# Two-layer hybrid encoder: the last head's result stays on chip, and attention gets its own large tiles

## The chip, the cores and the metric

The kernel runs on one core of one Trainium2 chip. The metric is the device time of one execution in microseconds (us); three timed runs of the kernel before gave 2697.81 as the median, 2691.86 and 2702.72 as the ends. The profile is of one further execution.

## The reference

The input `h` has 256 tokens of 2048 channels. Two layers are computed, each with its own float32 weights:

```
u = rmsnorm(h);  z = u @ w_in                        # 6528 columns, shared out among four mixers
mix = concat[A(z_A), B(z_B), C(z_C), D(z_D)]         # 4 x 512 channels
h += mix @ w_out                                     # 2048 x 2048
h += relu(rmsnorm(h) @ w_up)^2 @ w_down              # 2048 x 8192 and back
h += (p[i] @ w_ple) * sigmoid(rmsnorm(h) @ w_gate)
```

A is differential attention: 4 heads, two 256x256 softmax maps a head, queries and keys normed. B is a gated linear recurrence in both directions, 4 heads of 128 channels. C is mean pooling with windows 2, 4, 8 and 16 and a small linear map. D is RWKV-7 time mixing in both directions, 8 heads of 64.

## The kernel before

All activations lie transposed, channels on the 128 partitions and the 256 tokens along the free dimension, so 2048 channels are 16 chunks of 128x256. A chunk of the 16 that `w_out` multiplies is one mixer output: chunks 0 to 3 are A's heads, 4 to 7 B's, 8 to 11 C's, 12 to 15 D's pairs of heads. Below, A3 is head 3 of A, and so on.

**Matrix products.** Each is done in split form: a float32 operand becomes a rounded part and a remainder. `wsplit` (L142 to L146) loads 128x1024 weights into a tile `raw` by a DMA on SyncE's queue (SP), ScalarE copies them to `wh` (L144), VectorE subtracts to get `wl` (L146). `split` (L180, L181) does the same for an activation. TensorE then runs three products (`mm3`, L151 to L153) or, where one of 512 columns holds two, two (`mm2`, L158, L159).

**Stages of a layer.** `mixers` (L395) computes z block by block (`K.z`, 51 blocks of 128 columns; L227 takes each from PSUM) and the four mixers. In the text of the program come first D's first part for four pairs, `invert`, D's second part for pairs (1, 3), then (0, 2), and then for c = 0 to 3 C's group, A's head and B's head (`rest`). Each finished chunk goes to DRAM with `put` (L413, a DMA on SP's queue) into `o_scr`.

**`w_out`.** `MIX` lists the order of the 16 chunks. The first 12 are loaded back (`load_mix`, L270 into `ot`, then split into `mh`) and used by the first product (`w_out1`, 16 blocks of 12 chunks, L158 and L159 with `mh`; L162 and L163 add to `h`). The last 4 are used by a second product (`w_out2`, L151 to L153 with `mh`, added at L305), into a tile `mh2` that takes the place of `u1`, the input of the z blocks.

**Memory.** A pool is a stretch of on-chip memory with named tiles; tiles with one tag share the place and follow one another. `dp` and `ab` hold the mixers' tiles. A and B share tags in `ab`: A's `qn`, B's `bQ` and its queries are tag `bQ`; A's `L` and B's `bK` are `x22`; A's `ct` and B's `bAT` are `x21`; both `vt` are `x13`; A's raw keys and B's `sg` are `x11`. So A of head c+1 waits with these tiles for B of head c, and B of head c+1 for A of head c+1. A and B also share two PSUM banks (`K.pab`), D has four (`K.pds`). At block 9 of the first product (`m == 9`) `dp` and `ab` are closed and a pool `wide` takes their place, with three buffers each of `raw`, `wh` and `wl` for all blocks from there on; blocks 0 to 8 use four `raw` and two each of the others in pool `wp`. A tile of `wide` waits for the tiles that lay at its place.

**Order.** The instructions of each engine, and DMAs of SP's queue, are put in order when the program is built, by a planner that simulates times and takes what is ready, earlier program text first. On the chip each queue runs in this order; an instruction that waits holds up what is behind it in the same queue.

Of the kernel before, what the change touches and what calls it, by code (L numbers as in the profile page):

```python
# [8 lines left out]
F32 = mybir.dt.float32  # L9
F32R = mybir.dt.float32r  # L10
# [6 lines left out]
P = 128  # L17
# [33 lines left out]

POOL_W = (2, 4, 8, 16)

MIX = [8, 0, 4, 9, 1, 5, 10, 15, 2, 13, 6, 11, 14, 3, 12, 7]
NOUT1 = 12
A_OFF, H_OFF, C_OFF, R_OFF = 0, 1536, 4096, 4608

# [14 lines left out]
def trunk(ctx: ExitStack, tc: tile.TileContext, xT, pT, w_in, w_out1, w_out2, w_up, w_down, w_gate, w_ple, pvec,  # L72
# [182 lines left out]
    for l in range(DEPTH):  # L255
# [32 lines left out]
        for m in range(KC):  # L288
# [4 lines left out]
                K.raw_bufs, K.w_bufs = RAW_WIDE, W_WIDE  # L293
            ps = out_block(w_out1[l, m], mh1, NOUT1, mm2)
            add_to(h[:, m], ps)
        mh2 = K.up.tile([P, KC - NOUT1, 2 * S], F32R, tag="u1", name="mh2")
        mh2 = [mh2[:, k] for k in range(KC - NOUT1)]
        for k in range(NOUT1, KC):
            load_mix(mh2[k - NOUT1], k)
        pgw = wide.enter_context(tc.tile_pool(name="pgw", bufs=4, space=PSUM, reuse_waits="tile"))  # L300
        K.accum = lambda name: pgw.tile([P, 512], F32, tag="accw", name=name)
# [1 line left out]
        for m in range(KC):  # L303
            ps = out_block(w_out2[l, m], mh2, KC - NOUT1, mm3)
            V.tensor_tensor(h[:, m], h[:, m], ps[:, :S], ALU.add)  # L305
            split(u[:, m], h[:, m], pc(l, "mlpg", m))
        op_.__exit__(None, None, None)
        K.up_.__exit__(None, None, None)


# [84 lines left out]
def mixers(K):  # L395
    nc, tc, l, es = K.nc, K.tc, K.l, K.es
    df_ = tc.tile_pool(name="df", bufs=1, side="right", reuse_waits="tile")
    K.df = df_.__enter__()
    D = MixerD(K)
    if l == 0:  # L400
        nc.sync.dma_start(K.cst, K.consts)
    else:
        nc.sync.dma_start(K.hscr, K.h)
    dp = es.enter_context(tc.tile_pool(name="dp", bufs=1, reuse_waits="tile"))
    ab = es.enter_context(tc.tile_pool(name="ab", bufs=1, reuse_waits="tile"))
    pd = es.enter_context(tc.tile_pool(name="pd", bufs=1, space=PSUM, reuse_waits="tile"))
    K.dp, K.ab, K.pd = dp, ab, pd
    K.pds = lambda name: pd.tile([P, 512], F32, tag="m", name=name, bufs=D_BANKS)
    K.pab = lambda name: pd.tile([P, 512], F32, tag="n", name=name, bufs=6 - D_BANKS)
    oscr = nc.dram_tensor("o_scr_%d" % l, (KC, P, S), F32, kind="Internal").ap()  # L410

    def put(chunk, t):
        nc.sync.dma_start(oscr[chunk], t)  # L413
    K.put = put

    def rest(c, base):
        K.base = base
        mixer_c(K, c)
        if l == 0 and c == 0:
            prepare(K)  # L420
        mixer_a(K, c)
        mixer_b(K, c)
    for c in range(4):
        D.first(c, 3 + 3 * c)
    df_.__exit__(None, None, None)
    D.invert()
    d2_ = tc.tile_pool(name="d2", bufs=1, side="right", reuse_waits="tile")
    K.d2 = d2_.__enter__()
    for cs in ((1, 3), (0, 2)):
        D.second(cs)  # L430
    d2_.__exit__(None, None, None)
    for c in range(4):
        rest(c, 15 + 9 * c)
    return oscr
# [450 lines left out]
def mixer_c(K, gi):  # L885
    nc, tc, l, ab, pd = K.nc, K.tc, K.l, K.ab, K.pd
    V, A, G, T = nc.vector, nc.scalar, nc.gpsimd, nc.tensor
    PW = 8 + S + 8
    cw = ab.tile([P, P], F32, tag="cw", name="cw", bufs=2)
    nc.sync.dma_start(cw, K.cw[l, :, gi])  # L890
    zt = ab.tile([P, PW], F32, tag="zc", name="zc", bufs=1)
    G.memset(zt[:, 0:8], 0.0)
    G.memset(zt[:, 8 + S:], 0.0)
    K.z(K.base, zt[:, 8:8 + S])
    cur, lo_, n = zt, 0, PW

    for st in range(gi + 1):
        nxt = ab.tile([P, PW], F32, tag="zs", name="zs", bufs=2)
        a_, b_ = (1, 0) if st == 0 else (1 << (st - 1), 1 << (st - 1))
        lo2, n2 = lo_ + a_, n - a_ - b_  # L900
        G.tensor_tensor(nxt[:, lo2:lo2 + n2], cur[:, lo2 - a_:lo2 - a_ + n2], cur[:, lo2 + b_:lo2 + b_ + n2],
                        ALU.add)
        cur, lo_, n = nxt, lo2, n2
    dd = ab.tile([P, S], F32, tag="zd", name="zd", bufs=1)
    ic = ICN + gi * 16
    G.tensor_scalar(dd[:, 8:S - 8], cur[:, 16:S], 1.0 / POOL_W[gi], None, ALU.mult)
    G.tensor_tensor(dd[:, 0:8], cur[:, 8:16], K.cst[:, ic:ic + 8], ALU.mult)
    G.tensor_tensor(dd[:, S - 8:], cur[:, S:S + 8], K.cst[:, ic + 8:ic + 16], ALU.mult)
    G.tensor_tensor(dd, dd, zt[:, 8:8 + S], ALU.subtract)
    pw = K.pab("psc")  # L910
    T.matmul(pw[:, :S], cw, dd, start=True, stop=True)
    V.tensor_scalar(dd, pw[:, :S], K.pc(l, "cb", gi), K.pc(l, "cs", gi), ALU.add, ALU.mult)
    K.put(8 + gi, dd)


def mixer_a(K, h):
    nc, tc, l, ab, pd = K.nc, K.tc, K.l, K.ab, K.pd
    V, A, G, T = nc.vector, nc.scalar, nc.gpsimd, nc.tensor
    mat, pc, dcol = K.mat, K.pc, K.dcol

    def t1(tag="t1", bufs=3, name=None):
        return ab.tile([P, S], F32, tag=tag, name=name or tag, bufs=bufs)

    for x, gn in ((0, "aq"), (1, "ak")):
        t = t1("x1%d" % x, 1)
        K.z(K.base + 1 + x, t)
        sq = t1()
        A.activation(sq, t, AF.Square)
        p2 = K.pab("psa1")
        T.matmul(p2[:, :S], mat("bo64"), sq, start=True, stop=True)  # L930
        rs = t1()
        K.rsqrt(rs, p2[:, :S], K.eps_b)
        if x == 0:

            qn = ab.tile([P, 2, S], F32, tag="bQ", name="qn")
            for m in range(2):
                V.scalar_tensor_tensor(qn[:, m], t, pc(l, gn, m), rs, ALU.mult, ALU.mult)
        else:
            V.scalar_tensor_tensor(t, t, pc(l, gn), rs, ALU.mult, ALU.mult)
            kn = t  # L940
    vz = t1("z", 2)
    K.z(K.base + 3, vz)
    vt = t1("x13", 1)
    p2 = K.pab("psa2")
    for j in range(2):
        T.transpose(p2[:, j * P:(j + 1) * P], vz[:, j * P:(j + 1) * P], mat("ident"))
    A.activation(vt, p2[:, :S], AF.Copy)
    ct = ab.tile([P, 2, S], F32, tag="x21", name="ct", bufs=1)
    for qc in range(2):
        qs = slice(qc * P, (qc + 1) * P)  # L950
        L = ab.tile([P, 2, S], F32, tag="x22", name="L", bufs=1)
        for m in range(2):
            pl = K.pab("psl")
            T.matmul(pl[:, :S], qn[:, m, qs], kn, start=True, stop=True)  # L954
            V.scalar_tensor_tensor(L[:, m], pl[:, :S], 0.125, K.biast[:, h, P - qc * P:P - qc * P + S], ALU.mult, ALU.add)
        st = ab.tile([P, 8], F32, tag="st", name="st", bufs=2)
        V.tensor_reduce(st[:, 0:2], L, AX.X, ALU.max, negate=True)
        for m in range(2):
            A.activation(L[:, m], L[:, m], AF.Exp, bias=st[:, m:m + 1], accum_out=st[:, 2 + m:3 + m])
        V.reciprocal(st[:, 4:6], st[:, 2:4])  # L960
        V.tensor_tensor(st[:, 6:7], st[:, 5:6], dcol(l, 28), ALU.mult)
        A.activation(L[:, 0], L[:, 0], AF.Identity, scale=st[:, 4:5])
        V.scalar_tensor_tensor(L[:, 0], L[:, 1], st[:, 6:7], L[:, 0], ALU.mult, ALU.add)
        p2 = K.pab("psct")
        for kc in range(2):
            T.transpose(p2[:, kc * P:(kc + 1) * P], L[:, 0, kc * P:(kc + 1) * P], mat("ident"))
        A.activation(ct[:, :, qs], p2[:, :S].rearrange("p (a b) -> p a b", a=2), AF.Copy)
    po = K.pab("pso")
    for kc in range(2):
        T.matmul(po[:, :S], vt[:, kc * P:(kc + 1) * P], ct[:, kc, :], start=(kc == 0), stop=(kc == 1))  # L970
    t = t1()
    A.activation(t, po[:, :S], AF.Copy)
    sq = t1()
    A.activation(sq, t, AF.Square)
    p2 = K.pab("psan")
    T.matmul(p2[:, :S], mat("ones_v"), sq, start=True, stop=True)
    rs = t1()
    K.rsqrt(rs, p2[:, :S], K.eps_b)
    V.scalar_tensor_tensor(t, t, dcol(l, 19), rs, ALU.mult, ALU.mult)
    K.put(h, t)  # L980


def mixer_b(K, hd):
# [5 lines left out]
    def t1(tag="t1", bufs=3, name=None):  # L989
        return ab.tile([P, S], F32, tag=tag, name=name or tag, bufs=bufs)  # L990

    def v2(t):
        return t.rearrange("p (a b) -> p a b", a=2)
# [2 lines left out]
    F = ab.tile([P, 4 * W], F32, tag="bF", name="bF")  # L996
    Kt = ab.tile([P, 2, W], F32, tag="x22", name="bK")
    Q = ab.tile([P, 2, W], F32, tag="bQ", name="bQ")
    sg = t1("x11", 1)
    zq = t1("z", 2)  # L1000
    K.z(base, zq)
    K.sigmoid(q, zq)
# [33 lines left out]
    for li in range(7):  # L1036
# [6 lines left out]
        for i in range(2):  # L1043
            T.matmul(p2[:, i * P:(i + 1) * P], kc[:, i * P:(i + 1) * P],  # L1044
                     strided(Q, i * P, [[2 * hh, P // (2 * hh)], [W + hh, 2], [1, hh]]), start=True, stop=True)
        V.copy_predicated(ATd, K.lm[:, li * P:(li + 1) * P].unsqueeze(1).to_broadcast([P, 2, P]), v2(p2[:, :S]))
        fq = strided(F, off + 1, [[nb - 1, 2], [2, nb // 2], [0, hh]])
        fk = strided(F, off + nb + 1, [[-(nb + 1), 2], [2, nb // 2], [0, hh]])
        qv = strided(Q, 0, [[W + hh, 2], [2 * hh, nb // 2], [1, hh]])
        kv = strided(Kt, 0, [[W + hh, 2], [2 * hh, nb // 2], [1, hh]])  # L1050
        V.tensor_tensor(qv, qv, fq, ALU.mult)
        V.tensor_tensor(kv, kv, fk, ALU.mult)
        if li < 6:
            V.tensor_tensor(F[:, off + 2 * nb:off + 3 * nb], strided(F, off, [[2, nb]]),
                            strided(F, off + 1, [[2, nb]]), ALU.mult)
# [157 lines left out]
```

## Time and profile before

| | |
|---|---|
| median of 3 runs | 2697.81 us |
| the profiled execution, its time | 2694.64 us |
| its span, first to last instruction | 2692.9 us |
| TensorE (PE) busy | 2636.8 us, 98% |
| VectorE (DVE) busy | 1833.7 us, 68% |
| ScalarE (ACT) busy | 1440.1 us, 53% |
| mean granted TensorE clock | 0.994 |

Times in the rows count from the span's start. The mixers of the first layer end at about 481 us and those of the second at about 1812 us; `w_out` runs around these times. PE is a TensorE matmul, PEld a weight load, SPq an issue on SP's queue. A granted clock of 1.00 is 2.4 GHz, 0.50 is 1.2 GHz.

### The profile page before, as it was taken

The numbers are of one execution on the slowest core, as the hardware profiler recorded it, in microseconds if no ns is written. First come the engines' busy times: TensorE is split into PE (matmuls) and PEld (weight loads), VectorE is DVE, ScalarE is ACT, GpSimd is POOL, SyncE is SP. The second block draws the span as 40 slices with busy tenths as digits, with TensorE's granted clock in tenths as the row PEclk, the third lists the DMA queues.
The fourth block names the chain that finished last, engine by engine and source line by source line (L and its number), as shares of the span: only waits on it lengthen the run. The fifth ranks groups of instructions, "written<-read, shape, count | busy, mean of one in ns | idle before, by whom it ended". The sixth has DMA issues, their size and how long they took to land.

```text
span 2692.9 us, 46250 instructions
## 1 busy us (share of the span) xinstructions
PE 2636.8 (98%) x18150; PEld 2383.8 (89%) x18150; DVE 1833.7 (68%) x3033; ACT 1440.1 (53%) x2402; POOL 58.4 (2%) x86
## 2 busy tenths in 40 slices
PE   8999999899999999999999999989999999999999
PEld 7998998788888888888899999978888888888888
DVE  7897567676656666567777876667666566665676
ACT  7665455465535445345766655545554454453455
POOL 0000100000000000000000110100000000000000
PEclk9999999999999999999999999999999999999999
DMA  6764555566666556566557555546656565656565
GB/s 233 216 187 149 154 169 154 186 205 188 189 193 189 188 191 191 188 189 196 187 166 217 172 160 159 181 126 186 193 191 188 189 193 189 188 190 192 189 199 165
DMA packets 186386, 496.71 MB, mean 184 GB/s; under 512 B 46996, under 2 KB 66068, under 8 KB 186040
## 3 DMA queue, kind: packets, MB, share of 16 engines
q1 hardware_dynamic: 186168, 493.76, 58.4%
q8 instruction: 142, 2.33, 0.4%
q14 instruction: 76, 0.62, 0.1%
HBM read 474.01 MB, written 19.68 MB: 183 GB/s over the span
## 4 chain that ended last, share of the span: by engine, by line
PE 91%; DVE 4%; DMA 3%; ACT 2%; issue 1%; SPq 0%; DVEq 0%; ACTq 0%
PE acc L158 42%; PE acc L159 22%; PE acc L153 7%; PE acc L151 6%; PE acc L152 6%; DVE wl L146 2%; ACT wh L144 1%; DMA ot<-o_scr 1%; PE psbl L1044 1%; DMA raw<-in_w_out 1%; PE psam L602 1%; PE pss L766 1%; PE psl L954 0%; PE psy L801 0%; PE psr L757 0%
## 5 line engine op out<-in xcount | busy, mean ns | idle before, releaser
L144 ACT ACTIVATE wh<-raw 128x1024 fp32r<-128x1024 f32 (+1 forms) x884 | 909.1, 1029 | 1069.6 <-PE acc L158 810.5
L146 DVE TENSOR_TENSOR wl<-raw,wh 128x1024 fp32r<-128x1024 f32 (+1 forms) x884 | 1048.3, 1187 | 608.5 <-ACT wh L144 584.4
L158 PE MATMUL acc<-u,wh 128*128 128x512 f32 x2048 | 711.0, 392 | 0.4 <-ACT wh L144 0.2
L158 PE MATMUL acc<-act,wh 128*128 128x512 f32 x2048 | 710.2, 390 | 0.0
L159 PE MATMUL acc<-act,wl 128*128 128x256 f32 x2048 | 577.5, 282 | 0.0
L159 PE MATMUL acc<-u,wl 128*128 128x256 f32 x2048 | 572.3, 280 | 1.6 <-DVE wl L146 1.6
L151 PE MATMUL acc<-u,wh 128*128 128x256 f32 x1632 | 469.3, 288 | 12.3 <-ACT u L183 8.8
L153 PE MATMUL acc<-u,wl 128*128 128x256 f32 x1632 | 470.0, 288 | 5.8 <-DVE wl L146 5.4
L152 PE MATMUL acc<-u,wh 128*128 128x256 f32 x1632 | 466.1, 286 | 1.1 <-DVE u L184 0.9
L158 PEld LDWEIGHTS acc<-u,wh 128*128 128x128 f32 x2048 | 384.4, 188 | 85.6 <-ACT wh L144 0.8
L158 PEld LDWEIGHTS acc<-act,wh 128*128 128x128 f32 x2048 | 384.4, 188 | 80.6
L159 PEld LDWEIGHTS acc<-act,wl 128*128 128x128 f32 x2048 | 387.1, 189 | 0.0
L159 PEld LDWEIGHTS acc<-u,wl 128*128 128x128 f32 x2048 | 384.5, 188 | 2.3 <-DVE wl L146 2.2
L151 PEld LDWEIGHTS acc<-u,wh 128*128 128x128 f32 x1632 | 309.1, 189 | 17.4 <-ACT u L183 9.0
L153 PEld LDWEIGHTS acc<-u,wl 128*128 128x128 f32 x1632 | 308.8, 189 | 12.9 <-DVE wl L146 9.4
L152 PEld LDWEIGHTS acc<-u,wh 128*128 128x128 f32 x1632 | 308.7, 189 | 5.8 <-DVE u L184 2.2
L158 PE MATMUL acc<-ug,wh 128*128 128x512 f32 x512 | 179.5, 392 | 0.3 <-ACT wh L144 0.3
L158 PE MATMUL acc<-mh,wh 128*128 128x512 f32 x384 | 140.5, 404 | 16.2 <-ACT wh L144 16.2
L159 PE MATMUL acc<-ug,wl 128*128 128x256 f32 x512 | 143.6, 280 | 0.8 <-DVE wl L146 0.8
L162 DVE TENSOR_TENSOR h<-h,acc 128x256 f32<-128x256 f32 x160 | 67.3, 420 | 76.9 <-PE acc L159 75.1
L159 PE MATMUL acc<-mh,wl 128*128 128x256 f32 x384 | 113.5, 295 | 5.0 <-DVE wl L146 4.2
L158 PEld LDWEIGHTS acc<-ug,wh 128*128 128x128 f32 x512 | 96.1, 188 | 20.6 <-ACT wh L144 0.5
(295 smaller groups left out, 2551.2 us busy)
## 6 DMA issues: line engine op xcount, KB each, us to landing
raw<-in_w_up SPq DMA_DIRECT2D x256, 512.0 KB
raw<-in_w_down SPq DMA_DIRECT2D x256, 512.0 KB
raw<-in_w_in SPq DMA_DIRECT2D x204, 512.0 KB
raw<-in_w_gate SPq DMA_DIRECT2D x64, 512.0 KB
raw<-in_w_out SPq DMA_DIRECT2D x32, 512.0 KB
raw<-in_w_out SPq DMA_DIRECT2D x64, 256.0 KB
h<-in_xT SPq DMA_DIRECT2D x8, 512.0 KB
ot<-o_scr SPq DMA_DIRECT2D x32, 128.0 KB
```

The source lines that it names most:

```text
L144: A.activation(wh[:, :cols], raw[:, :cols], AF.Copy)
L146: V.tensor_tensor(wl[:, :cols], raw[:, :cols], wh[:, :cols].bitcast(F32), ALU.subtract)
L151: T.matmul(ps[:, :S], w1, act[:, :S], start=start, stop=False)
L152: T.matmul(ps[:, :S], w1, act[:, S:], start=False, stop=False)
L153: T.matmul(ps[:, :S], w2, act[:, :S], start=False, stop=stop)
L158: T.matmul(ps, w1, act, start=start, stop=False)
L159: T.matmul(ps[:, :S], w2, act[:, :S], start=False, stop=stop)
L162: V.tensor_tensor(dst, dst, ps[:, S:], ALU.add)
L602: T.matmul(pm[h][:, j * P:(j + 1) * P], BK[HS[h], j].rearrange("p a b -> p (a b)"), KS[HS[h], j].rearrange("p a b -> p (a b)"), start=True ...
L766: T.matmul(pss[0:64, o:o + 64], TT[p][0:64, d, h * 4 + js[d]], R[0:64, p, d * P + h * 64:d * P + (h + 1) * 64], start=(p + d + h == 0), st ...
L1044: T.matmul(p2[:, i * P:(i + 1) * P], kc[:, i * P:(i + 1) * P], strided(Q, i * P, [[2 * hh, P // (2 * hh)], [W + hh, 2], [1, hh]]), start=T ...
```

## The change

1. `MIX` gets another order: the first 12 chunks are now 8, 0, 9, 4, 1, 13, 15, 10, 5, 2, 12, 14, the last four 11, 6, 3, 7. So chunks 12 and 14 move to the first product, 6 and 11 to the second. The rows of `w_out` are laid out in this order.
2. `put` of the last chunk (7, B3) makes no DMA: it takes tile `mh2` there and then, and splits the chunk straight into its last quarter. The other three are loaded as before.
3. For heads 1 to 3, A's `qn`, `vt`, `ct` and `L` come from a pool `ax` of their own (7 KB a partition on the other side of the memory, opened after `invert`). B's `sg` gets a tag of its own. A3 takes its PSUM banks from D's four.
4. C's `dd` shares tag `zs`.
5. In B's loop over 7 levels, the keys are multiplied first, then the queries, and the predicated copy of the scores comes last.

```
-MIX = [8, 0, 4, 9, 1, 5, 10, 15, 2, 13, 6, 11, 14, 3, 12, 7]
+MIX = [8, 0, 9, 4, 1, 13, 15, 10, 5, 2, 12, 14, 11, 6, 3, 7]
...
-        mh2 = K.up.tile([P, KC - NOUT1, 2 * S], F32R, tag="u1", name="mh2")
-        mh2 = [mh2[:, k] for k in range(KC - NOUT1)]
-        for k in range(NOUT1, KC):
+        mh2 = [K.mh2[:, k] for k in range(KC - NOUT1)]
+        for k in range(NOUT1, KC - 1):
             load_mix(mh2[k - NOUT1], k)
...
     def put(chunk, t):
-        nc.sync.dma_start(oscr[chunk], t)
+        if chunk == MIX[-1]:
+
+            K.mh2 = K.up.tile([P, KC - NOUT1, 2 * S], F32R, tag="u1", name="mh2")
+            K.split(K.mh2[:, KC - NOUT1 - 1], t)
+        else:
+            nc.sync.dma_start(oscr[chunk], t)
...
+    K.ax_ = tc.tile_pool(name="ax", bufs=1, side="right", reuse_waits="tile")
+    K.ax = K.ax_.__enter__()
...
-    dd = ab.tile([P, S], F32, tag="zd", name="zd", bufs=1)
+    dd = ab.tile([P, PW], F32, tag="zs", name="zd", bufs=2)[:, :S]
...
+    if h == 0:
+        own = lambda shape, tag, old, name: ab.tile(shape, F32, tag=old, name=name, bufs=1)
+    else:
+        own = lambda shape, tag, old, name: K.ax.tile(shape, F32, tag=tag, name=name)
+    pab = K.pds if h == 3 else K.pab
...
-            qn = ab.tile([P, 2, S], F32, tag="bQ", name="qn")
+            qn = own([P, 2, S], "aqn", "bQ", "qn")
...
-    vt = t1("x13", 1)
+    vt = own([P, S], "avt", "x13", "vt")
...
-    ct = ab.tile([P, 2, S], F32, tag="x21", name="ct", bufs=1)
+    ct = own([P, 2, S], "act", "x21", "ct")
...
-        L = ab.tile([P, 2, S], F32, tag="x22", name="L", bufs=1)
+        L = own([P, 2, S], "aL", "x22", "L")
...
-    sg = t1("x11", 1)
+    sg = t1("sg", 1)
...
-        V.copy_predicated(ATd, K.lm[:, li * P:(li + 1) * P].unsqueeze(1).to_broadcast([P, 2, P]), v2(p2[:, :S]))
...
+        V.tensor_tensor(kv, kv, fk, ALU.mult)
         V.tensor_tensor(qv, qv, fq, ALU.mult)
-        V.tensor_tensor(kv, kv, fk, ALU.mult)
+        V.copy_predicated(ATd, K.lm[:, li * P:(li + 1) * P].unsqueeze(1).to_broadcast([P, 2, P]), v2(p2[:, :S]))
```

## Rows read from the trace of the kernel before

**Rows 1.** Windows around block 9: us, busy us (instructions) by engine, clock, DMA.

```profile
478.70:487.60 8.90, 0.02 (x1) 0.00 (x0) 2.48 (x5) 2.40 (x5) 0.00 (x0) 0.73 0.82 281
487.60:493.10 5.50, 5.01 (x15) 3.93 (x16) 3.39 (x4) 1.90 (x3) 0.00 (x0) 0.50 0.64 199
...
1810.70:1818.00 7.30, 0.07 (x1) 0.07 (x1) 1.35 (x4) 2.01 (x4) 0.00 (x0) 0.73 0.54 169
1818.00:1825.00 7.00, 6.54 (x21) 5.27 (x22) 3.56 (x5) 2.47 (x4) 0.00 (x0) 0.55 0.57 198
1825.00:1835.00 10.00, 10.00 (x60) 8.85 (x59) 6.79 (x11) 4.45 (x5) 0.00 (x0) 1.00 0.48 159
```

**Rows 2.** Timeline, first layer, end of B3: start, us, engine, line [idle before].

```profile
480.92 0.42 DVE L1073 TENSOR_TENSOR t<-t,x 128x256 f32<-128x256 f32 x1
481.38 0.33 SPq L413 DMA_DIRECT2D o_scr<-t  x1
481.75 1.42 SPq L142 DMA_DIRECT2D raw<-in_w_out  x3
486.52 1.61 ACT L144 ACTIVATE wh<-raw 128x1024 fp32r<-128x1024 f32 x2 [6.47 <-DMA raw<-in_w_out]
487.63 0.79 PE L158 MATMUL acc<-mh,wh 128*128 128x512 f32 x1 [8.91 <-ACT wh L144]
488.89 0.58 PE L159 MATMUL acc<-mh,wl 128*128 128x256 f32 x1 [0.47 <-DVE wl L146]
```

**Rows 3.** Timeline, SP's queue around the put, first layer, then second layer.

```profile
467.69 13.16 SPq L142 DMA_DIRECT2D raw<-in_w_in  x6
...
1783.77 12.24 SPq L142 DMA_DIRECT2D raw<-in_w_out  x6
1812.95 1.40 SPq L142 DMA_DIRECT2D raw<-in_w_out  x3
```

**Rows 4.** Waits of SP's queue, 1790 to 1830 us: total, times, longest us.

```profile
SPq L413 <- DVE t L1073: 16.5, 1, 16.5
```

**Rows 5.** Chain of waits, A3 and B3 of the first layer: start, us.

```profile
409.29 0.43 PE psa L930 x2
...
439.71 1.13 PE pso L970 x4
445.77 0.71 PE psbd L1031 x4
```

**Rows 6.** One line's instructions, 385 to 432 us, then 410 to 550 us.

```profile
L227 DVE TENSOR_TENSOR z<-acc,rstd x6: 417/425/425, 395.1 to 428.3; 128x256 f32<-128x256 f32 x6
...
L162 DVE TENSOR_TENSOR h<-h,acc x16: 410/418/422, 435.1 to 520.0; 128x256 f32<-128x256 f32 x16
```

**Rows 7.** Lines, whole span: busy us, mean ns, idle before.

```profile
L181 DVE TENSOR_TENSOR mh<-ot,mh 128x256 fp32r<-128x256 f32 x32 | 13.4, 440 | 6.9 <-ACT mh L180 6.9
L1046 DVE COPY_PREDICATED bAT<-lm,psbl 128x256 f32<-128x256 uint8 x56 | 25.0, 446 | 20.7 <-PE psbl L1044 20.3
L180 ACT ACTIVATE mh<-ot 128x256 fp32r<-128x256 f32 x32 | 12.3, 413 | 12.4 <-DMA ot<-o_scr 12.4
```

**Rows 8.** One line's instructions, whole span: D's finished chunks.

```profile
L822 DVE TENSOR_TENSOR t<-t,bg x8: 402/410/416, 313.0 to 1722.4; 128x256 f32<-128x256 f32 x8
```

**Rows 9.** Window while the first product runs beside B3.

```profile
455.00:465.00 10.00, 9.59 (x58) 8.22 (x57) 8.02 (x18) 4.16 (x7) 0.00 (x0) 1.00 0.46 146
```

**Rows 10.** Waits, TensorE, whole span.

```profile
PE acc L159 <- DVE wl L146: 6.5, 11, 1.3
...
PE psbl L1044 <- DVE bQ L1051: 1.0, 1, 1.0
```

**Rows 11.** Window of 50 us while D's second part starts, first layer.

```profile
200.00:250.00 50.00, 46.60 (x478) 44.23 (x477) 35.82 (x78) 23.53 (x47) 3.16 (x3) 0.93 0.53 159
```

**Rows 12.** Timeline, end of B3 in the second layer.

```profile
1812.12 0.42 DVE L1073 TENSOR_TENSOR t<-t,x 128x256 f32<-128x256 f32 x1
1819.19 0.58 PE L159 MATMUL acc<-mh,wl 128*128 128x256 f32 x1 [0.46 <-DVE wl L146]
```

More of the change, by code (lines that the diff above doesn't have):

```diff
@@ L307, in trunk @@
         op_.__exit__(None, None, None)
+        K.ax_.__exit__(None, None, None)
         K.up_.__exit__(None, None, None)
@@ L928, in mixer_a @@
         A.activation(sq, t, AF.Square)
-        p2 = K.pab("psa1")
+        p2 = pab("psa1")
         T.matmul(p2[:, :S], mat("bo64"), sq, start=True, stop=True)
@@ L942, in mixer_a @@
     K.z(K.base + 3, vz)
-    vt = t1("x13", 1)
-    p2 = K.pab("psa2")
+    vt = own([P, S], "avt", "x13", "vt")
+    p2 = pab("psa2")
     for j in range(2):
@@ L947, in mixer_a @@
     A.activation(vt, p2[:, :S], AF.Copy)
-    ct = ab.tile([P, 2, S], F32, tag="x21", name="ct", bufs=1)
+    ct = own([P, 2, S], "act", "x21", "ct")
     for qc in range(2):
         qs = slice(qc * P, (qc + 1) * P)
-        L = ab.tile([P, 2, S], F32, tag="x22", name="L", bufs=1)
+        L = own([P, 2, S], "aL", "x22", "L")
         for m in range(2):
-            pl = K.pab("psl")
+            pl = pab("psl")
             T.matmul(pl[:, :S], qn[:, m, qs], kn, start=True, stop=True)
@@ L963, in mixer_a @@
         V.scalar_tensor_tensor(L[:, 0], L[:, 1], st[:, 6:7], L[:, 0], ALU.mult, ALU.add)
-        p2 = K.pab("psct")
+        p2 = pab("psct")
         for kc in range(2):
@@ L967, in mixer_a @@
         A.activation(ct[:, :, qs], p2[:, :S].rearrange("p (a b) -> p a b", a=2), AF.Copy)
-    po = K.pab("pso")
+    po = pab("pso")
     for kc in range(2):
@@ L974, in mixer_a @@
     A.activation(sq, t, AF.Square)
-    p2 = K.pab("psan")
+    p2 = pab("psan")
     T.matmul(p2[:, :S], mat("ones_v"), sq, start=True, stop=True)
```

## The prediction, made before the run

> **What bounds the kernel now.** I read the page first: TensorE is busy 98% of the span, so a change can only win what TensorE idles or runs slowly, and the sums below count that alone. The windows came next. Outside the mixers and `w_out` they stand at 100%; the one deep hole in either layer lies at block 9 of the first product [rows 1]. The reader is to see two things there: 8.90 us with 0.02 us of matmul in the first layer and 7.30 us with 0.07 us in the second, and after each hole 5.5 to 7 us at a granted clock of 0.50 and 0.55, that is 1.2 GHz, before 1.00 is back.
>
> The timeline says what TensorE waits for [rows 2]. VectorE ends B3's result at 481.34 (480.92 + 0.42), SP issues its put at 481.38, and only then, at 481.75, three weight loads for block 9, back to back. ScalarE has waited 6.47 us for the first of them, TensorE 8.91 us for ScalarE. The waits of SP's queue show the same in the second layer [rows 4]: the put held the queue for 16.5 us, until L1073 was done, with the three loads behind it. The loads issue back to back right behind the put [rows 2, 3], so when the put went nothing else held them.
>
> The chain of waits shows why B3 is so late [rows 5]: A3 runs from 409.29 to 439.71, and B3's first scores (psbd) follow at 445.77; its last instruction, L1073, is the one of [rows 2]. The two run one after the other because they share tiles. The last of the z blocks that feed them was taken from PSUM at 428.3 [rows 6], so B3 starts 17 us after the last z, and by shared tiles, not for want of input.
>
> **The change, part by part.**
>
> *The put of the last chunk.* It takes one issue of 0.33 us from SP's queue, the load of the same chunk, and the hold of the loads behind. Second layer: SP had nothing to do from 1796.0 (the six issues begin at 1783.77 and take 12.24 us [rows 3]) until the put; without it the three loads issue some 17 us earlier, and land well before TensorE needs them at 1810.7. First layer: the six issues end at 480.85 (467.69 + 13.16 [rows 3]), 0.9 us before the loads at 481.75, so there the put alone is worth 0.9 us. What would help there is that B3 ends before block 9 is reached, so that the planner opens the pool `wide` earlier and puts its loads ahead of those six.
>
> *A's own tiles.* They take A3 out of the line in front of B3. B3's chain from psbd to L1073 took 35.6 us (445.77 to 481.34 [rows 2, 5]). It needs the z of its gates, two z blocks before the last; six z in 33.2 us are 6.6 us apart [rows 6], so these are in by 415. I give the gates 7 us: psbd at 422, L1073 at about 458, 23 us earlier. How far is the first product by then? Block 0 is added at 435.1 [rows 6] and block 8 is done at the hole, 478.7: 5.4 us a block, with A3 and B3 between. At 458 it is in block 5, and some 20 us stand between B3's end and block 9; 15 us, as A3's matmuls no longer lie in them. For the second layer I assume the same lengths, since its hole lies at the same block.
>
> *What both give.* At full pace 60 instructions take 10 us, 0.167 us each [rows 1]. First layer: 14.4 us (8.90 + 5.50) hold 16 instructions, worth 2.7 us, so 11.7 us are lost. Second layer: 14.3 us hold 22, worth 3.7, so 10.6 us are lost. Sum 22.3 us.
>
> *What is late next.* A3's and B3's work on VectorE now falls in a shorter time beside the blocks' own. VectorE was at 8.02 of 10 us beside B3 [rows 9]; a weight part `wl` that comes late makes TensorE wait, at most 1.3 us so far [rows 10]. I take one such wait more in each layer, 2.6 us; the ends are nothing, as A3 can move ahead of the first product, and 5 us a layer: B3's 35.6 us at 8.02 of 10 are 28.6 us of VectorE, half of A3's 30.4 us (409.29 to 439.71) at the same share 12.2, together 5 us more than the 35.6.
>
> *The split on chip* has the two instructions that the loaded chunk had (0.41 us on ScalarE, 0.44 on VectorE [rows 7]), earlier. Nothing is added: the four last chunks are used only after block 15, at 520.0 [rows 6].
>
> *The new order of chunks.* The first product now needs 12 and 14, D's last. Their last instruction ran at 1722.4 in the second layer [rows 8]; block 9 stood at 1810.7, nine blocks of 5.4 us after the product's start, which puts that at 1762, 39 us later. A put and a load back are two transfers of 128 KB, estimated at under 10 us from the 4.8 us that a load of 512 KB took (481.75 to 486.52 [rows 2]). They stay hidden under z blocks. Chunks 6 and 11 move to the end, which frees the first product from B2 and C3: no cost, and TensorE can take a block where a z is held up.
>
> *B's loop.* The predicated copy (0.446 us [rows 7]) leaves the path between scores and next queries, 7 x 0.45 = 3.1 us for B3's chain. It is counted at nothing, as B3 is then 15 us ahead of what needs it; without that slack it gives 3.1 us a layer. *C's tag, the new tag for `sg`, the pool `ax`, A3's banks* add no instruction. What they could cost is a wait for the tiles below, for which no row exists: nothing at the low end, as D's first part is long over when A1 starts, and one hole like that of 200 to 250 us (3.40 us idle [rows 11]) at the high end; the nearest to it, TensorE's waits beside B, are nothing, so I take nothing.
>
> *Gain elsewhere.* As D's second part starts in the first layer 3.40 us are idle, and a mean clock of 0.93 over 50 us is 7 us at half speed, worth at most 3.5 us more [rows 11]. A beside B gives TensorE more to choose from there: 0 to 7 us. I take 0, since its queue runs in the planned order whatever is ready.
>
> The sum: 2694.64 - 22.3 + 2.6 = 2674.9 for the profiled execution. The median of the runs lies 3.17 us above it (2697.81), so I predict 2678.
>
> **Rivals.**
>
> *Only the hold on SP goes; the order on VectorE stays.* The block's first `wl` stays behind L1073 in VectorE's queue. It would start at 481.34, and take the 1.26 us by which TensorE's second matmul came after its first (487.63 to 488.89 [rows 2]): TensorE goes on at 482.6, 6.3 us earlier; in the second layer at 1812.54 + 1.26 = 1813.8 instead of 1819.19 [rows 12], 5.4 us. The gain is 11.7 us. If the shorter hole leaves the clock up, 5.6 us more (the second windows of [rows 1], 12.5 us with 36 instructions worth 6.0 us and 0.9 us of waits for `wl`): 2681 to 2686. For it: TensorE waited for that `wl` too, 0.47 and 0.46 us [rows 2, 12]. Against it: a B3 that ends 23 us earlier is planned at another place. The Trainium skill ("TensorE: Matmul & The Clock Gate", Part 1, Architectural detail) says that ScalarE and VectorE are strict first-in first-out while TensorE can pull weight loads ahead; it speaks against counting on the engines to slip past B3's tail. The trace agrees as far as it shows: `wl` never started ahead of L1073 there.
>
> *Only the second layer gains.* If A's tiles don't shorten the chain (two PSUM banks still serve A and B), the put is worth 0.9 us in the first layer and 10.6 in the second: 2686.
>
> *The change doesn't do what it says.* The loads of block 9 may be waiting for B3's own tiles, which end with the same instruction as the put's input; the trace cannot tell the two. Then nothing but the put's issue goes: 2697.
>
> *Slower.* The planner writes A's matmuls of head c+1 between B's levels of head c, on two banks and the same VectorE queue; the true chain is slower than the simulated (SP stood 16.5 us at the put in the planned order [rows 4]), and TensorE waits in order at each level. Place: psbl of B0 to B2, 7 levels each, both layers, 42 levels. Price: at each what the one such wait of before took, 1.0 us [rows 10]: 42 us, less the 20 won: 2720. It decides from 0.5 us a level on. Against it: of the 56 levels of before one showed such a wait.
>
> **How the numbers follow.** The forecast gets 0.53, the order on VectorE 0.14, one layer alone 0.12, no effect 0.09, slower 0.12. Half a per cent is 13.5 us, about what a measurement here can tell from none: faster is below 2684.3, slower above 2711.3. Faster: 0.53 and half of 0.14, 0.60. Slower: 0.10 of its 0.12. Same: the rest, 0.30. The forecast's own range is 2668 (7 us elsewhere, no new wait) to 2685 (5 us a layer of waits for VectorE). The range for 8 in 10 reaches up over the one layer and the no-effect case to 2700, and down to 2664, as the median of a few runs moves by some 4 us itself (2691.86 to 2702.72 before).
>
> **What would show it.** Right: no TensorE wait above 2 us for `wh` at block 9 in either layer; no granted clock below 0.9 between the mixers and the end of `w_out`; SP's loads for block 9 issued before B3's last instruction or long before they are needed; psbd of B3 within 5 us of the last z; A3 beside B2. Wrong: a hole that has only moved (to block 9 with another releaser, or in front of the second product), more idle at psbl, or VectorE above 9 of 10 us beside B3 with TensorE waiting for `wl`.

## The result and the profile after

| | before | after |
|---|---|---|
| median of 4 runs | 2694.89 us | 2666.71 us |
| lowest and highest | 2691.86, 2702.72 | 2661.82, 2668.06 |
| ratio of after to before, 95% | | 0.9898 [0.9886, 0.9909] |
| profiled execution, time | 2694.64 us | 2668.06 us |
| its span | 2692.9 us | 2666.3 us |
| TensorE busy | 2636.8 us | 2628.4 us |
| mean granted TensorE clock | 0.994 | 0.997 |

The kernel became 28.2 us faster, 1.0%; the forecast was 2678 us, 19.8 us below the 2697.81 that it started from (the median of the first three runs; with a fourth it is 2694.89). The profiled spans differ by 26.6 us. Of these, 8.4 us are less busy time of TensorE (the same 18150 instructions run more of their time at full clock) and 18.2 us less idle time (56.1 us before, 37.9 after).

The windows around block 9 of the first product, which in the kernel after starts at about 470.7 us in the first layer and 1794 us in the second; the columns are those of [rows 1].

```profile
466.00:470.70 4.70, 4.70 (x28) 4.17 (x28) 3.21 (x5) 1.86 (x2) 0.00 (x0) 1.00 0.89 313
470.70:474.50 3.80, 3.80 (x23) 3.37 (x23) 2.94 (x6) 1.33 (x3) 0.00 (x0) 1.00 0.87 278
474.50:484.50 10.00, 10.00 (x59) 8.86 (x59) 7.01 (x11) 4.00 (x5) 0.00 (x0) 1.00 0.73 216
1786.00:1790.50 4.50, 2.06 (x11) 1.35 (x10) 3.69 (x5) 3.71 (x5) 0.00 (x0) 1.00 0.28 88
1790.50:1794.50 4.00, 4.00 (x25) 3.53 (x24) 2.09 (x4) 0.00 (x0) 0.00 (x0) 1.00 0.53 175
1794.50:1804.50 10.00, 10.00 (x60) 8.86 (x59) 5.86 (x9) 3.39 (x4) 0.00 (x0) 1.00 0.40 112
```

Where [rows 1] had 8.90 and 7.30 us with almost no matmul and then half clock, TensorE is now busy throughout at 1.00. What is left is the fourth line, 2.44 us idle as block 8 starts in the second layer. The waits of TensorE over the span of the kernel after, in us: total, times, longest.

```profile
PE acc L151 <- ACT u L183: 7.7, 1, 7.7
PE acc L159 <- DVE wl L146: 6.7, 10, 1.0
PE acc L153 <- DVE wl L146: 3.9, 7, 1.0
PE psW L719 <- DMA U<-x_scr: 3.9, 3, 2.1
PE acc L151 <- ACT wh L144: 2.0, 4, 0.9
PE psa L943 <- ACT t L941: 1.9, 1, 1.9
PE acc L158 <- ACT wh L144: 1.7, 2, 1.4
```

The seventh line is the one that mattered: the wait for `wh` at L158 was 16.8 us before, with the 8.91 us of [rows 2] and 7.33 us of the second layer in it, and is 1.7 now. Waits for `wl` (second and third lines) total 10.6 us; before they were 6.5 [rows 10] and 5.4. The chain of waits of the kernel after, first layer, then second (start, us), answers to [rows 5]:

```profile
404.24 0.43 PE psa L943 x2
...
418.45 0.45 PE psbd L1044 x4
438.18 0.86 PE pso L983 x4
...
1741.02 0.45 PE psbd L1044 x4
1749.58 0.87 PE pso L983 x4
```

B3's first scores (psbd) now come before A3's end (pso) in both layers, 418.45 before 438.18; in [rows 5] they came 6 us behind it. The lines' instructions say when z, B3 and the product run: the last z block, B3's last multiply (the first layer alone, then all eight heads of both layers, of which the last is B3's of the second), and the blocks of the first product in each layer; first and last start.

```profile
L227 DVE TENSOR_TENSOR z<-acc,rstd x6: 414/425/425, 387.9 to 421.5; 128x256 f32<-128x256 f32 x6
...
L1086 DVE TENSOR_TENSOR t<-t,sg x2: 424/426/427, 403.5 to 456.6; 128x256 f32<-128x256 f32 x2
L1086 DVE TENSOR_TENSOR t<-t,sg x8: 424/424/427, 228.8 to 1779.2; 128x256 f32<-128x256 f32 x8
...
L162 DVE TENSOR_TENSOR h<-h,acc x16: 409/417/422, 429.0 to 499.1; 128x256 f32<-128x256 f32 x16
L162 DVE TENSOR_TENSOR h<-h,acc x16: 412/418/422, 1749.9 to 1823.2; 128x256 f32<-128x256 f32 x16
```

B3 ends at 457.0 in the first layer (481.34 before [rows 2]) and at 1779.6 in the second (1812.54 [rows 12]). The stretch from the first to the last of the 16 blocks is 70.1 us against 84.9 [rows 6], and 73.3 us against 85.1 in the second layer (1765.6 to 1850.7 before): 14.8 + 11.8 = 26.6 us, as much as the spans differ. Windows of these stretches, the kernel before and then the kernel after:

```profile
435.10:520.00 84.90, 74.08 (x412) 63.67 (x411) 52.79 (x98) 37.38 (x61) 0.00 (x0) 0.94 0.56 178
1765.60:1850.70 85.10, 74.96 (x414) 64.42 (x414) 52.71 (x100) 35.22 (x58) 0.00 (x0) 0.94 0.45 141
```

```profile
429.00:499.10 70.10, 68.14 (x394) 59.32 (x393) 48.34 (x85) 33.66 (x53) 0.00 (x0) 1.00 0.66 208
1749.90:1823.20 73.30, 69.31 (x397) 60.00 (x396) 46.52 (x84) 30.20 (x46) 0.00 (x0) 1.00 0.52 158
```

The 26.6 us are of three kinds. TensorE idles 6.0 us in the two stretches instead of 21.0: 15.0 us. The half clock behind the holes is gone: the 5.01 and 6.54 us busy at half clock in [rows 1] held 15 and 21 instructions, worth 6.0 us at full pace, so 5.5 us. And the stretches hold 18 and 17 instructions fewer, worth 5.8 us at 0.167 us each: they are mostly B3's first matmuls, which now run before the first block is added. This last part is work that moved and is not saved by itself. Outside the two stretches the sum is nearly nothing: the first product starts 6.1 us earlier in the first layer, although more work lies ahead of it, as TensorE idles 13.9 us there instead of 20.1; the stretch from its end to the start of the second layer's is 5.1 us longer, and the rest of the kernel 0.9 us longer.

### The profile page after: what moved, and what is told of

Read it like the earlier page. It is cut to its first block, busy times and chain, and to the rows that moved or that the text cites. A ratio compares the mean times of both kernels' runs of the same rounds, so it can differ in the third digit from the quotient of the medians.

```text
span 2666.3 us, 46180 instructions
## 1 busy us (share of the span) xinstructions
PE 2628.4 (99%) x18150; PEld 2381.3 (89%) x18150; DVE 1834.9 (69%) x3033; ACT 1439.4 (54%) x2402; POOL 57.5 (2%) x86
## 4 chain that ended last, share of the span: by engine, by line
PE 92%; DMA 3%; DVE 3%; ACT 1%; issue 1%; SPq 0%; POOL 0%; DVEq 0%; ACTq 0%; POOLq 0%
PE acc L158 42%; PE acc L159 22%; PE acc L153 7%; PE acc L151 7%; PE acc L152 7%; DVE wl L146 1%; PE psbl L1057 1%; DMA raw<-in_w_out 1%; ACT wh L144 1%; PE psam L610 1%; PE pss L774 1%; DMA ot<-o_scr 1%; PE psl L967 0%; PE psr L765 0%; PE psw L556 0%
## 5 line engine op out<-in xcount | busy, mean ns | idle before, releaser
L158 PE MATMUL acc<-u,wh 128*128 128x512 f32 x2048 | 711.3, 392 | 0.1
L158 PE MATMUL acc<-act,wh 128*128 128x512 f32 x2048 | 710.2, 390 | 0.0
L158 PEld LDWEIGHTS acc<-u,wh 128*128 128x128 f32 x2048 | 384.4, 188 | 85.4 <-ACT wh L144 0.7
L158 PEld LDWEIGHTS acc<-act,wh 128*128 128x128 f32 x2048 | 384.4, 188 | 80.6
L158 PE MATMUL acc<-ug,wh 128*128 128x512 f32 x512 | 179.4, 392 | 0.3 <-ACT wh L144 0.3
L158 PE MATMUL acc<-mh,wh 128*128 128x512 f32 x384 | 136.3, 395 | 1.4 <-ACT wh L144 1.4
L158 PEld LDWEIGHTS acc<-ug,wh 128*128 128x128 f32 x512 | 96.1, 188 | 20.6 <-ACT wh L144 0.5
```

The source lines that it names most:

```text
L158: T.matmul(ps, w1, act, start=start, stop=False)
```

## The experiments

Times are medians of timed runs; each ratio is to runs of the kernel before taken beside them (medians of 2691.5 to 2694.0), with its 95% interval. Medians of one and the same kernel thus differ by up to 2.5 us between these sets. The holes are TensorE's longest wait for `wh` at block 9 in the first and second layer (8.91 and 7.33 us before).

### The put through DRAM again, all else changed

```
-        if chunk == MIX[-1]:
-
-            K.mh2 = K.up.tile([P, KC - NOUT1, 2 * S], F32R, tag="u1", name="mh2")
-            K.split(K.mh2[:, KC - NOUT1 - 1], t)
-        else:
-            nc.sync.dma_start(oscr[chunk], t)
+        nc.sync.dma_start(oscr[chunk], t)
```

> The changed kernel, but chunk 7 (B3) goes to DRAM and back as before. Theory 'B3 ends sooner' (A's own tiles take A3 out of the line in front of B3, so the pool wide opens sooner): no hole at block 9 in either layer, 2666 to 2671 us, within 4 us of the changed kernel. Theory 'the put' (the put holding SP's queue is what makes the hole): the hole is back in both layers, 2683 to 2690 us.

2666.11 us, 0.9892 [0.9876, 0.9907]: as the changed kernel. Neither layer has a hole; in the first product of the first layer TensorE has no wait but 1.8 us in three for `wl`. So once B3 is early, keeping its result on chip is worth nothing that shows.

### The split on chip alone, on the kernel before

```
-        for k in range(NOUT1, KC):
+        for k in range(NOUT1, KC - 1):
...
-        nc.sync.dma_start(oscr[chunk], t)
+        if chunk == MIX[-1]:
...
+            K.split(K.mh2[:, KC - NOUT1 - 1], t)
+        else:
+            nc.sync.dma_start(oscr[chunk], t)
```

> The kernel before, with only the on-chip split of chunk 7 (no put, no load of it). 'B3 ends sooner': the first layer keeps its hole of 7 to 9 us, since the put held the loads there for 0.9 us only; the second layer's hole of 7.3 us shrinks to under 3 us; 2683 to 2687 us. 'The put': both holes go, 2672 to 2676 us.

2689.58 us, 0.9982 [0.9973, 0.9991], some 3 us above the expected band, with holes of 7.89 and 3.38 us, the second just above the 3 us that were expected at most. The timeline of this kernel at the second layer's hole (start, us, engine, line, [idle before]):

```profile
1808.74 0.42 DVE L1077 TENSOR_TENSOR t<-t,x 128x256 f32<-128x256 f32 x1
1809.20 0.42 ACT L180 ACTIVATE mh<-t 128x256 fp32r<-128x256 f32 x1 [1.01 <-DVE t L1077]
1809.52 2.51 ACT L144 ACTIVATE wh<-raw 128x1024 fp32r<-128x1024 f32 x3
```

SP now issued the three loads at 1792.69 to 1793.63, against 1812.95 in [rows 3], as argued; TensorE still waited 3.38 us. ScalarE's `wh` stands in its queue behind the new split (L180), which waits for B3's last instruction (L1077). The hold moved from SP's queue to ScalarE's: the rival "Only the hold on SP goes; the order on VectorE stays", on the neighbouring engine. The Trainium skill ("TensorE: Matmul & The Clock Gate", Part 1, Architectural detail) calls ScalarE strictly first-in first-out; the two rows agree, `wh` starting 0.32 us after the start of L180 and not before.

### A's tiles and banks alone, on the kernel before

The `ax` tiles, `sg`'s and `dd`'s tags and A3's banks of the change; put, order of chunks and B's loop as before.

```
+    if h == 0:
+        own = lambda shape, tag, old, name: ab.tile(shape, F32, tag=old, name=name, bufs=1)
+    else:
+        own = lambda shape, tag, old, name: K.ax.tile(shape, F32, tag=tag, name=name)
+    pab = K.pds if h == 3 else K.pab
...
-    sg = t1("x11", 1)
+    sg = t1("sg", 1)
```

> The kernel before, with only A's own tiles (pool ax, own tag for sg, A3 on D's banks, C's dd in zs); the put, MIX and B's loop as before. 'B3 ends sooner': B3's first scores come within 10 us of the last z, no hole at block 9, 2668 to 2676 us. 'The put': both holes stay, 2690 to 2696 us.

2668.31 us, 0.9898 [0.9881, 0.9915], as the changed kernel (0.9898 [0.9886, 0.9909]). This part gives all of the gain that the noise lets one see; `dd` in `zs` was not tried apart from it. The chain of waits of this kernel, B3's scores before A3's end again:

```profile
423.99 0.45 PE psbd L1040 x4
439.58 0.86 PE pso L979 x4
```

### The order of chunks alone, and B's loop alone, on the kernel before

The first edit is the change's `MIX`, the second the new order of the three VectorE instructions in B's loop.

```
+MIX = [8, 0, 9, 4, 1, 13, 15, 10, 5, 2, 12, 14, 11, 6, 3, 7]
...
-        V.copy_predicated(ATd, ...
         V.tensor_tensor(kv, kv, fk, ALU.mult)
         V.tensor_tensor(qv, qv, fq, ALU.mult)
+        V.copy_predicated(ATd, ...
```

> The kernel before, with only the new order of the 16 chunks. Both theories: B3 ends as late as before and the holes stay, 2690 to 2698 us. A third, 'the first product starts sooner' (it no longer needs B2 and C3, and TensorE fills its gaps with blocks): 2683 to 2688 us.

> The kernel before, with only B's loop in the new order (keys, queries, then the predicated copy). As predicted, it gives nothing by itself as long as nothing waits for B3; but here B3 still is what block 9 waits for, so its chain shortens by 7 x 0.45 = 3.1 us a layer at most: 2688 to 2694 us, holes of 7 to 9 us still there. If the loop were a large part of the gain: under 2680 us.

The order alone: 2688.68 us, 0.9978 [0.9969, 0.9987], holes of 8.46 and 3.38 us. The loop alone: 2685.91 us, 0.9973 [0.9961, 0.9984], holes of 9.82 and 4.10 us. Both are 1 to 2 us below the bands in which the holes stay. Both leave the first layer's hole and halve the second's, as the split alone did. With the new order the second layer's put goes at 1805.99 instead of 1812.5, 2 us before block 8 is done. Three unlike edits thus shorten the same hole by 3 to 4 us each, so what they give alone is not to be added up. They don't do it by the same means. Counted from the first block's add in the second layer, B3 ends after 46.9 us in the kernel before and after 47.0 with the split alone, so there the earlier loads did it; with the order or the loop alone it ends after 41.2 and 40.8 us, so there an earlier B3 did it, still with its put.

### The tiles without the banks, and the banks without the tiles

```
-    pab = K.pds if h == 3 else K.pab
+    pab = K.pab
```

> The kernel before, with A's own tiles, but A3 keeps the two PSUM banks that it shares with B. Theory 'tiles' (the shared tiles are what put A3 ahead of B3): as with the tiles and D's banks, 2666 to 2672 us, no holes. Theory 'tiles and banks' (two banks also put A3 and B3 one behind the other, so both are needed): B3's first scores follow A3's last product again, holes of 7 to 9 us in both layers, 2686 to 2694 us.

> The kernel before, with only A3 on D's four PSUM banks; all tiles shared as before. Theory 'banks' (the two banks alone put A3 ahead of B3): 2666 to 2674 us, no holes. Theory 'tiles and banks': holes stay, 2686 to 2694 us.

Tiles without banks (this edit on the kernel with A's tiles and banks alone): 2684.82 us, 0.9969 [0.9957, 0.9981], holes of 9.73 and 3.54 us. Banks alone (`pab` as in the change, in the kernel before): 2690.28 us, 0.9992 [0.9983, 1.0002], holes of 9.95 and 3.83 us. The chain of waits of the kernel with tiles and without banks:

```profile
436.58 1.13 PE pso L979 x4
442.65 0.71 PE psbd L1040 x4
```

And that of the kernel with the banks alone:

```profile
438.24 0.86 PE pso L971 x4
441.89 0.45 PE psbd L1032 x4
```

B3 stands behind A3 again, by the 6 us of [rows 5] with the tiles alone and by 3.7 us with the banks alone. Own tiles don't let B3 start while the two heads still take turns at two PSUM banks; own banks don't while they share tiles. One line is worth 2684.82 - 2668.31 = 16.5 us, given the tiles. Both kernels fit the theory 'tiles and banks' (the first 1.2 us below its band), except that the second layer's hole shrinks to 3.5 and 3.8 us, as it did with the split, the order and the loop alone. The trace of the kernel before had named the bank (start, us, engine, line, [idle before]):

```profile
445.25 0.47 ACT L188 ACTIVATE t<-psan,cbias 128x256 f32<-128x256 f32 x1
445.77 0.52 PEld L1031 LDWEIGHTS psbd<-x,bkc 128*128 128x128 f32 x4 [0.42 <-ACT t L188]
```

What B3's first scores waited for last was ScalarE reading `psan`, the PSUM tile of A3's final norm, and not a tile in `ab`.

### Own tiles for the last head alone

```
-    if h == 0:
+    if h < 3:
```

> The kernel before, with own tiles and D's banks for A3 alone; A1 and A2 share B's tiles as before (with C's dd in zs and sg's own tag, as in all kernels with the tiles). Theory 'pool': only B3's end counts, so the same as with the tiles for heads 1 to 3, 2666 to 2671 us. If A1 and A2 beside B0 and B1 are worth something: 2672 to 2680 us.

2678.22 us, 0.9944 [0.9929, 0.9959], about 7 us above the band of theory 'pool' and inside the other. The holes are gone. The first block is added at 439.0 in the first layer, against 434.7 with all of A's tiles. TensorE's wait for `wh`, 405 to 425 us, of this kernel and then of the one with all of A's tiles, and a window behind it, of this kernel:

```profile
PE acc L151 <- ACT wh L144: 2.2, 1, 2.2
```

```profile
PE acc L151 <- ACT wh L144: 0.9, 1, 0.9
```

```profile
421.00:429.00 8.00, 6.73 (x35) 6.48 (x35) 5.59 (x16) 4.11 (x10) 0.00 (x0) 0.57 0.34 99
```

The other three waits there (for `wl`, A3's `t` and a z, 3.4 us) are the same in both kernels. Here the wait for `wh` is 1.3 us longer, and behind it the clock falls to half for 6.8 us, worth 3.4 us; in the other kernel it stays at 1.00. The two are about the later start of 4.3 us. So A1's and A2's own tiles matter too, some 10 us against the kernel with all of A's tiles; why `wh` comes later, and the rest of the 10 us, no run tells.

### The pool at block 12, on the kernel before and on the changed kernel

```
-            if m == 9:
+            if m == 12:
```

> The kernel before, with one constant changed: the pool wide opens at block 12 of the first product instead of block 9. Nothing of B3's chain changes. Theory 'pool' (what costs time is that block 9 is the first with weights in the mixers' memory, which opens when B3 ends): blocks 9 to 11 run on, the holes are gone, 2666 to 2674 us with B3 as late as before. Theory 'late B3' (B3's tail itself stops the engines): holes of over 5 us stay about where B3 ends, 2685 to 2696 us.

> The changed kernel, with the pool wide opened at block 12 instead of 9. Theory 'pool': with B3 done at block 6 nothing waits for the opening any more, so the constant that gave 12 us to the kernel before gives nothing here, 2663 to 2670 us. If the late opening helped the kernel before for another reason (the loads spread out better): 2654 to 2660 us.

On the kernel before: 2680.92 us, 0.9953 [0.9938, 0.9968], with B3 as late as ever (its last multiply at 474.7, 45.4 us after the first block's add; before 45.8). If the hole is B3's end against the opening of the pool, moving the opening must close it; it does, though the time stays 7 us above the expected band. Windows of this kernel, first layer:

```profile
482.20:485.70 3.50, 0.49 (x1) 0.19 (x1) 3.33 (x5) 3.37 (x6) 0.00 (x0) 1.00 0.96 365
485.70:490.00 4.30, 4.29 (x16) 3.72 (x17) 2.36 (x4) 0.00 (x0) 0.00 (x0) 0.60 0.91 302
```

Of the hole, two waits are left as block 11 starts, 1.66 us for `wh` and 1.37 us for `wl`, with the DMA engines 0.91 to 0.96 busy: SP sends the put at 475.13 and behind it, by 480, three loads for `w_out` (two of 512 KB, one of 256) and two for the next layer; ScalarE waits 3.63 us for the first of them, and the clock falls once. The put still holds the loads of the opened pool, as in [rows 2]. Block 11 does not need these, but its `wh` stands behind theirs in ScalarE's queue: its own loads had landed by 477.9, and ScalarE copies it at 482.76, third after the wait that ends at 481.27. On the changed kernel: 2672.15 us, 0.9931 [0.9915, 0.9948], 2 us above the expected band and slower than with block 9. TensorE's waits, 440 to 500 us, of this kernel, and 420 to 505 us of the changed kernel with block 9:

```profile
PE acc L159 <- DVE wl L146: 4.5, 6, 1.0
```

```profile
PE acc L159 <- DVE wl L146: 2.0, 3, 1.0
```

Blocks 9 to 11 now stay with two buffers of `wh` and `wl`, and TensorE waits for `wl` six times instead of three. While B3 was late, the late opening gained 12 us, of which the profiles place 10.8 in the two products (79.1 and 80.1 us instead of 84.9 and 85.1); with B3 early it costs 5 (73.7 and 75.0 us instead of 70.1 and 73.3).

### The new order of chunks in the first layer alone

On the changed kernel, with the rows of `w_out` laid out by layer.

```
+MIX = [[8, 0, 9, 4, 1, 13, 15, 10, 5, 2, 12, 14, 11, 6, 3, 7],
+       [8, 0, 4, 9, 1, 5, 10, 15, 2, 13, 6, 11, 14, 3, 12, 7]]
...
+            nc.sync.dma_start(t, oscr[MIX[l][k]])
```

> The changed kernel, but the new order of chunks in the first layer alone; the second layer has the old one. In the profiles the stretch from the end of the first layer's first product to the first block of the second layer's took 1250.7 us with the new order and 1245.1 us with the tiles alone. Theory 'order' (the new order costs this in the second layer): 2660 to 2664 us. Theory 'execution' (such 5 us come and go between executions, by what the clock does after a DMA wait): within 2 us of the changed kernel, 2665 to 2669 us.

2660.18 us (2659.12 to 2662.54), 0.9880 [0.9865, 0.9895]: the lowest median of all, faster than the kernel before; against the changed kernel (2661.82 to 2668.06) the two intervals still meet. One window of the second layer's mixers, of the changed kernel, then of this one:

```profile
1716.00:1724.00 8.00, 5.34 (x27) 4.64 (x26) 4.73 (x8) 5.37 (x12) 0.00 (x0) 0.79 0.72 203
```

```profile
1716.00:1724.00 8.00, 8.00 (x66) 7.79 (x65) 6.52 (x13) 7.11 (x16) 0.00 (x0) 1.00 0.65 198
```

The changed kernel waits 1.87 us there for A's `t` (psa, L943) and then runs 3.4 us at half clock; with the old order in this layer neither is there, and the stretch between the two products is 1245.7 us against 1250.7. But this wait is not what the new order brings each time: the changed kernel with the put through DRAM and the one with the pool at block 12 have the new order in both layers, no such wait, and stretches of 1251.3 and 1247.5 us. What these three share is a wait of 2.0 or 2.1 us for the DMA of `U` in the second layer's mixers (the 2.1 us in the waits of the kernel after); this kernel and the one with A's tiles and banks alone have none there.

### That kernel with B's loop in its old order

```
+        V.copy_predicated(ATd, ...
-        V.tensor_tensor(kv, kv, fk, ALU.mult)
         V.tensor_tensor(qv, qv, fq, ALU.mult)
-        V.copy_predicated(ATd, ...
+        V.tensor_tensor(kv, kv, fk, ALU.mult)
```

> The kernel with the new order of chunks in the first layer alone (2660.18 us), with B's loop in the old order (copy, queries, keys). Theory 'nothing' (B3 ends at block 6 and nothing waits for it, so its chain may be longer): 2658 to 2663 us. Theory 'loop' (the loop still shortens what TensorE waits for beside B): 2664 to 2668 us.

2666.22 us, 0.9905 [0.9888, 0.9921]: 6.0 us more by the medians and 4.2 by the profiled spans, with intervals that just meet. TensorE's waits of this kernel, 378 to 420 us, before the first layer's product, and those of the kernel with the new loop:

```profile
PE acc L152 <- ACT wh L145: 1.5, 1, 1.5
PE psa L944 <- ACT t L942: 1.3, 1, 1.3
PE acc L154 <- DVE wl L147: 1.2, 1, 1.2
PE acc L152 <- DVE z L228: 0.8, 1, 0.8
```

```profile
PE acc L152 <- DVE z L228: 0.5, 1, 0.5
PE acc L154 <- DVE wl L147: 0.4, 1, 0.4
```

4.8 us of waits against 0.9, and the first block is added 2.1 us later. The old order doesn't make B3 late again (its last multiply at 460.9); the z blocks beside B2 and A3 get their weights later. If the 4 to 6 us are more than noise, the loop was worth something at a place where no hole had been.

## Why the prediction was right, and what was off

**What bounds the kernel now** held. The two holes and the half clock behind them were what could be won, and they gave 20.5 of the 26.6 us between the spans.

**The put of the last chunk** was the wrong carrier of the gain. By itself it left 7.89 us of the hole in the first layer, where its price was put at 0.9 us, which fits; in the second layer the 17 us earlier loads came as foretold, but of the 10.6 us only part, as `wh` was then held on ScalarE. In the changed kernel it gives nothing (2666.11 without it, 2666.71 with it).

**A's own tiles** came out nearly to the number: psbd at 418.45 where 422 was put, B3's end at 457.0 where about 458 was, in block 6 of the first product where block 5 was put, and 24 us earlier than before. That the times fit to 4 us is in part luck: the whole stage ran some 7 us ahead (last z at 421.5, before 428.3), B3's scores came 3.1 us before the last z where 6.3 was put, and its chain took 38.5 us where 35.6 was put. What failed there is the account of the cause, "they share tiles" alone. "C's tag, the new tag for `sg`, the pool `ax`, A3's banks" were said to add no instruction and were passed over; the banks carry 16.5 us of the gain, since without them the tiles leave B3 behind A3. And "A3 beside B2", named as a sign, did not come: A3 starts at 404.24, behind B2's last norm at 400.57. It is B3 that runs beside A3.

**What both give** and **What is late next** came out well: 22.3 - 2.6 = 19.7 us was put, and idle time and half clock in the products gave 15.0 + 5.5 = 20.5. The new waits came too, if not quite as put: in the two stretches the waits for `wl` went from 3.3 to 4.2 us, and 1.41 us for `wh` as block 8 starts in the second layer is new, 2.3 us together.

**Gain elsewhere** was the term that was off: 0 was taken out of 0 to 7, and some 6 us came, 26.6 less 20.5. TensorE idles 6.2 us less ahead of the first product, so that the work that moved there didn't lengthen it; the window of [rows 11] has only 1.6 us of it (48.24 us busy instead of 46.60, at the same clock of 0.93). The second layer has no such gain. How much of it is the change's own can't be told from one execution; the last section shows why.

**The sum** has a second part that was off. The median, 2666.71, lies in the range for 8 in 10 but 1 us below the forecast's own range of 2668 to 2685. Of the 11 us between it and 2678, 7 lie between the profiled executions (2674.9 put, 2668.06 measured). The other 4.5 are the step from the profile to the median: 3.17 us were added, because the median of three runs lay that far above the profiled execution; with a fourth run it lay 0.25 us above, and the changed kernel's lies 1.35 us below.

**B's loop**, counted at nothing because B3 would be ahead of need, was perhaps mis-sized too: 4 to 6 us in the best kernel, with intervals that just meet. The slack of B3 said nothing of the z blocks and weights that queue on VectorE beside it.

**The new order of chunks**, counted at nothing, is nothing in the sum: alone 5 us better by a hole that any edit shortened, and in the changed kernel's second layer rather a loss, since the kernel with it in the first layer alone has the lower median and not the wait for `U`; the intervals still meet.

**The rivals.** "Only the second layer gains" was mistaken on the changed kernel, but its condition, two banks that still serve A and B, is the kernel with tiles and without banks: 2684.82. That its price was 2686 is luck, as it was worked out from a put that goes, and in that kernel the put stays. "The order stays" was seen, on ScalarE, in the second layer of the split alone. For "Slower" nothing showed: no wait at B's levels (psbl) is left. "The change doesn't do what it says" fell with the split alone, whose loads went some 15 us before B3's last instruction (1793.63 and 1808.74): they had been held by the put, and not by B3's tiles.

## What to carry to other kernels

Where two heads run one after the other, list everything that they share, tiles and PSUM banks alike, and free all of it at once: here the tiles alone gained 8 us, the banks alone nothing clear of noise, and both 26. Look behind the transfer that seems to hold a queue for what makes its input late: with B3 early the transfer cost nothing, and with B3 late its replacement held the next queue. And an edit costed at nothing because its own chain has slack may still matter through what shares its engine's queue.

## What the runs showed of the hardware that was not expected

After a wait of the same length the clock fell in one execution and not in another. The kernel before and the one that only opens the pool at block 12 wait, in D's second part of the first layer, for the same DMA (`U`), 2.2 and 2.1 us, with the same instructions in TensorE's queue up to the end of B3. Windows of the kernel before and then of that one:

```profile
225.00:245.00 20.00, 17.00 (x213) 15.43 (x211) 9.38 (x19) 9.06 (x22) 1.89 (x2) 0.83 0.63 171
```

```profile
225.00:245.00 20.00, 16.88 (x233) 15.24 (x232) 11.48 (x22) 10.46 (x25) 1.89 (x2) 1.00 0.64 180
```

The first ran 6.8 us at 1.2 GHz behind that wait, and again 3.4 us at 305 behind a wait of 1.5 us for a DMA (`sp`); the second stayed at 2.4 GHz behind the same wait, had no second one, and is 5.8 us ahead by 405 us. So a difference of some 6 us ahead of the products can stand between two executions of one order of TensorE's instructions. The 6.1 us by which the changed kernel starts its first product earlier are not all of this kind. In the same window it too ran 6.8 us at half clock:

```profile
225.00:245.00 20.00, 18.24 (x205) 17.32 (x203) 9.92 (x18) 11.97 (x27) 1.89 (x2) 0.83 0.72 206
```

It lacks only the second fall, 3.4 us and so 1.7 us of time, and the wait of 1.5 us in front of it. And the four kernels that share its first layer (the changed kernel itself, and with the put through DRAM, the pool at block 12, or the new order in the first layer alone) add their first block at 429.0 to 429.6.
